# RWKV-7 products grouped by shape, heads in turn, with hand-over points between the groups

## The chip, the cores and the metric

The kernel runs on one core of one Trainium2 chip. The metric is device time in microseconds (us), as the median of repeated runs; smaller is better. TensorE (PE in the profile) multiplies matrices, VectorE (DVE) and ScalarE (ACT) work on elements, SyncE (SP) issues most DMAs.

## The reference, cut to what matters

A decoder trunk of two layers works on 1024 tokens of width 1024 in float32. Layer 0 mixes with gated linear attention and S5, layer 1 with RWKV-7 (8 heads of 64) and Mamba-2; each layer also has an input projection, an output projection and a gated MLP with a short convolution. The change is in RWKV-7 alone, whose recurrence is:

```python
def step(S, inp):
    rt, wt, kt, vt, at, bt = inp
    sa = jnp.einsum('bhij,bhj->bhi', S, at)
    S = S * wt[:, :, None, :] + sa[..., None] * bt[:, :, None, :] + vt[..., None] * kt[:, :, None, :]
    return S, jnp.einsum('bhij,bhj->bhi', S, rt)
```

## The kernel before, in words

The tokens are worked on in two halves of 512 (`h` = 0, 1). The layer products (projections and MLP, `fm_tile`, `project`) are made as three float32r products of a high and a low part each, 128x128 weights by 512 columns; they write to the four `acc` slots of PSUM. Each weight unit of 12 such products is followed by `tick(2.56)`.

The mixers are Python generators which run beside the layer products. `tick` (line 279) adds 2.56 us times a rate (0.7 for RWKV and Mamba) to a credit `due`, and lets the generator make steps, each up to its next `yield`, until the VectorE work that the steps traced (`cost`, counted in `tt`, `ts` and `stt` alone) has used up the credit. A step that has no such work costs nothing and is followed by the next in the same tick. `both` (line 228) advances two mixers together. This sets the program order; the framework that builds the program then puts the instructions of each engine into an order of its own, by their place in the program and by what is ready in its own reckoning, so that layer products fill in where a mixer's product would wait. Weight splitting and the evacuation of layer products carry a high priority.

RWKV-7 works on pairs of heads (4 pairs per half, 8 in all), tokens in 8 chunks of 64. `rwkv_pair` (line 1238) runs in this order:

- values without their mean into `SAV`, one product for the bonus (lines 1243 to 1255);
- the pairwise products inside a chunk (lines 1257 to 1268): per head and per half of the chunks (`q`) four products of 64 rows, 128 weight columns and 128 moving columns into one PSUM slot, then a masked copy by VectorE and a plain `yield`; head 0 first, then head 1;
- transposes, the inverse (30 VectorE steps), and `PV`;
- the recurrence over 8 chunks (lines 1292 to 1327): per chunk `pR`, `pS` and `pZ`, two products each, each answered by a small VectorE step;
- the output products (lines 1328 to 1335): per chunk and head one product of 128 rows by 64 columns (`SAV`, `Ph`) and one of 64 by 64 (`Zs`, `AR`), both added into the same place;
- squares and a copy by ScalarE, the sums over a head (`hsel`), a reciprocal root by way of DRAM, and the gate product `g2` (lines 1338 to 1358).

While a pair runs, `rwkv_prep` of the next runs with it in `both`. The mixers' PSUM slots are the four of `mx`. Every float32 product is two passes on TensorE, and so two matmul records in the trace.

Of the kernel before, what the change touches and what calls it, by code (L numbers as in the profile page):

```python
# [73 lines left out]

class Arena:
    """Fixed slots handed out in program order, the one that was freed first before the others."""
# [21 lines left out]
    def same(self, t, view):  # L98
        """Another view of a slot, which it is freed by from now on."""
        self.held[id(view)] = (self.held.pop(id(t))[0], view)  # L100
        return view
# [8 lines left out]
class Ring:  # L110
    """Fixed slots in turn."""
# [11 lines left out]
class Kernel:  # L123
    def __init__(self, ctx, tc, a, dump=None):
# [5 lines left out]
        # What the activation engine has just written, it also sends off.  # L130
# [68 lines left out]
    def paid(self, out):  # L199
        """Counts the vector engine's work, by which the mixers are traced among the products."""  # L200
        self.cost += 0.06 + float(np.prod(out.shape[1:])) / 960
# [26 lines left out]
    def both(self, a, b):  # L228
        """Two mixers in turn; the second's result."""
        left, res = [a, b], None  # L230
        while left:
            keys = []
            for g in list(left):
                try:
                    keys.append(next(g))
                except StopIteration as e:
                    left.remove(g)
                    if g is b:
                        res = e.value
            if keys:  # L240
                yield None if None in keys else keys[0]
        return res

    def staggered(self, gens, lead):
        """Mixers one after the other, each begun when the one before has made its first steps."""
        gens, live = list(gens), []
        while gens or live:
# [9 lines left out]
            if keys:  # L257
                yield None if None in keys else keys[0]
# [4 lines left out]
    def stats_beside(self, h):  # L263
        """The statistics of a norm in steps among the products that follow."""
# [14 lines left out]
    def tick(self, us):  # L279
        """After us of products: what runs beside them goes on by its share."""  # L280
# [7 lines left out]
        while self.side is not None and self.due > 0:  # L288
            c = self.cost
            try:  # L290
                if next(self.side) is not None:
# [3 lines left out]
                self.side = None  # L295
            self.due -= self.cost - c

    def drain(self):
        if self.side is not None:
            for key in self.side:  # L300
                assert key is None, key
# [5 lines left out]
    def tr(self, out, in_, shifted=False):  # L307
        """Transpose; to PSUM partitions that don't start at 0, a product with the identity."""
# [112 lines left out]
    def rsqrt_rows(self, src, scale, bias, op1):  # L421
        """(src scale op1 bias)^-1/2 of rows in PSUM, left in DRAM: spread over the partitions on the way."""
# [13 lines left out]
    def rows_to(self, t, rows):  # L436
        """Loads each row on its share of the partitions."""
# [5 lines left out]
    def norm_stats(self, h, t0=0, n=T, get=None, far=False):  # L443
        """1 / rms of n tokens, on every partition (far: spread there through DRAM) and with tokens on partitions."""
# [67 lines left out]
    def project_final(self, h, srcs, w, k0, nk):  # L512
        """The last products: half of the tokens first, so that their norm runs beside the others."""
# [32 lines left out]
    def ffn(self, h, l, at=None, mid=None):  # L546
        a = self.a
        last = h == NH - 1 and l == 1
        if last:
            # The first products don't wait for the norm: its factor comes with their results.  # L550
# [52 lines left out]
    def gla_decays(self, h, wa2, alo):  # L603
        """Cumulated log decays (times 16) inside each chunk."""
# [10 lines left out]
        # This one comes after every exponential: the logarithms then share one load of their table.  # L615
# [168 lines left out]
    def s5_prep(self):  # L784
# [72 lines left out]
        # phase table  # L857
# [29 lines left out]
        for half in range(2):  # L887
            hs = slice(4 * half, 4 * half + 4)
            power = lambda x, i: x[:, hs, i:i + 1].to_broadcast([128, 4, SC])
            # input matrices: transpose of A^{7-j} B'  # L890
# [14 lines left out]
            # output matrices C A^i (real part and minus the imaginary part), i = 1..8  # L905
# [7 lines left out]
            # kernels C A^tau B' and their Toeplitz matrices  # L913
# [28 lines left out]
    def s5(self, h):  # L942
# [23 lines left out]
        for ri in range(2):  # L966
            v = self.k2([128, 8, SN + 1])
            V.tensor_copy(v[:, :, 0], self.s5X[ri])
            # conj(phase) * V
# [80 lines left out]
    def proj0(self, h, at, mid):  # L1050
        a = self.a
        w = a["w0fm"]
        if h == 0:
            # The first products don't wait for the norm: its factor comes with their results.
# [34 lines left out]
    def proj0_vg(self, h, hd, xs):  # L1089
        """Values and gates of a head, tokens on partitions; with head 0 the forget gates' low rank."""  # L1090
# [34 lines left out]
    def gla(self, h):  # L1125
        a = self.a
        yield from self.need(("gla", h, 0))
        # [high, low, high] parts of the weights against [high, high, low] parts of the low rank
# [30 lines left out]
    def rwkv_keys(self, h):  # L1159
        """The keys, and the factors that normalise them."""  # L1160
# [13 lines left out]
    def rwkv_prep(self, h, pr, tw, rk):  # L1174
# [5 lines left out]
        # decay  # L1180
# [25 lines left out]
        # in-context rate  # L1206
# [7 lines left out]
        # keys  # L1214
# [14 lines left out]
        # receptance  # L1229
# [8 lines left out]
    def rwkv_pair(self, h, pr, sg, prep):  # L1238
# [3 lines left out]
        # The values go in without their mean over the head: the recurrence keeps it away from the outputs too.  # L1242
# [13 lines left out]
        # pairwise products inside a chunk  # L1256
        Ph = []
        for hh in range(2):
            P = self.k4([128, C8, 128])
            hs = slice(64 * hh, 64 * hh + 64)  # L1260
            for q in range(2):
                ps = self.mx([128, 4, 128])
                for c in range(4):
                    self.mm(ps[:, c], BK[hs, 4 * q + c].rearrange("p a b -> p (a b)"), AR[hs, 4 * q + c].rearrange("p a b -> p (a b)"))
                self.tt(P[:, 4 * q:4 * q + 4], ps, self.rwmask.unsqueeze(1).to_broadcast([128, 4, 128]), MUL)
                self.fr(ps)
                yield
            Ph.append(P)
# [18 lines left out]
        # recurrence over the chunks  # L1287
# [4 lines left out]
        for c in range(C8):  # L1292
# [34 lines left out]
            yield  # L1327
        ps = self.mx([128, C8, RC])
        for c in range(C8):
            z0 = h == 0 and c == 0  # L1330
            for hh in range(2):
                hs = slice(64 * hh, 64 * hh + 64)
                self.mm(ps[hs, c], SAV[:, c, hs], Ph[hh][:, c, 64:128], stop=z0)
                if not z0:
                    self.mm(ps[hs, c], Zs[hs, c], AR[hs, c, 1], start=False)
        self.fr(Zs, SAV, AR, BK, PV, *Ph)
        yield
# [4 lines left out]
        yield  # L1342
# [4 lines left out]
        yield  # L1347
# [12 lines left out]
    def rwkv_inverse(self, Ph):  # L1360
        """Writes (I - A)^-1 over the strictly triangular A in the blocks [0:64, c, 0:64] of Ph."""
# [61 lines left out]
    def conv4(self, h, i):  # L1423
        """Causal convolution and twice the SiLU of it."""
# [13 lines left out]
    def proj1_dt(self, h, xs):  # L1438
        """Step sizes before their bias: rows by the weights' high and by their low parts."""
# [50 lines left out]
    def decays(self, h, hd, p0=0, p1=128):  # L1490
        """Log decays of a head from the start of each chunk, on every partition."""
# [357 lines left out]
```

## Time and profile before

| what | value |
|---|---|
| median of 3 runs | 2851.04 us (2846.32 to 2853.56) |
| span of the profiled execution | 2840.4 us |
| TensorE busy | 2765.3 us (97%) |
| VectorE busy | 1857.5 us (65%) |
| ScalarE busy | 1133.0 us (40%) |
| mean granted TensorE clock | 0.968 |

Busy time is the time in which an engine had at least one instruction in work. [...] The span runs from the first to the last instruction; what lies around it (10.6 us between the span and the median) is outside the trace.

### The profile page before, as it was taken

How to read it: one execution, taken by the hardware profiler on the slowest of the kernel's cores; microseconds unless marked ns; L12 is line 12 of the kernel's file. 1: busy time of each engine (PE TensorE's matmuls, PEld its weight loads, DVE VectorE, ACT ScalarE, POOL GpSimd, SP SyncE). 2: the span in 40 equal slices, each digit the busy share in tenths (PEclk: the TensorE clock that was granted, in tenths of full speed). 3: DMA queues.
4: the chain of work that ended last, by engine and by line, in shares of the span. 5: the costliest groups of instructions: out<-in, count | busy, mean ns of one | idle time of the engine just before them, and what ended most of it. 6: DMA issues, size and time to landing. Idle time of an engine off the chain costs nothing.

```text
span 2840.4 us, 40016 instructions
## 1 busy us (share of the span) xinstructions
PE 2765.3 (97%) x14172; PEld 2178.2 (77%) x14172; DVE 1857.5 (65%) x4440; ACT 1133.0 (40%) x2035; POOL 2.1 (0%) x6
## 2 busy tenths in 40 slices
PE   8999999999999999999999899999999989999998
PEld 6878888888788776867776686867677677888886
DVE  6986378664557564848466775657575577767566
ACT  4553355442334333424234553333232354443333
POOL 0000000000000000000000000000000000000000
PEclk9999899998999999999999999999999999999998
DMA  6545554433334542424233455424232244434332
GB/s 214 183 144 165 161 161 119 121 96 122 100 101 141 178 134 78 127 68 110 70 80 117 115 163 173 134 79 116 77 94 74 73 127 133 135 99 124 97 97 86
DMA packets 275377, 339.79 MB, mean 120 GB/s; under 512 B 97764, under 2 KB 133284, under 8 KB 275176
## 3 DMA queue, kind: packets, MB, share of 16 engines
q1 hardware_dynamic: 274944, 337.07, 40.3%
q8 instruction: 111, 1.82, 0.3%
q14 instruction: 90, 0.74, 0.1%
q10 hardware_dynamic: 232, 0.17, 0.0%
HBM read 286.91 MB, written 49.63 MB: 118 GB/s over the span
## 4 chain that ended last, share of the span: by engine, by line
PE 65%; DMA 4%; DVE 3%; ACT 1%; issue 1%; SPq 0%; ACTq 0%; DVEq 0%
PE acc L305 54%; PE mx L305 11%; DMA k<-dr 3%; DVE k L218 1%; ACT k L204 1%; DVE wl L208 0%; PE mx L312 0%; DVE k L208 0%; DVE x L208 0%; DVE kf L218 0%; DMA dr<-sm 0%; DMA dr<-k 0%; DMA yl<-dr 0%; ACT wh L204 0%; DMA rb<-dr 0%
## 5 line engine op out<-in xcount | busy, mean ns | idle before, releaser
L204 ACT ACTIVATE wh<-wr 128x512 fp32r<-128x512 f32 (+1 forms) x802 | 496.2, 620 | 931.2 <-PE acc L305 781.5
L208 DVE TENSOR_TENSOR wl<-wr,wh 128x512 fp32r<-128x512 f32 (+1 forms) x800 | 540.5, 677 | 450.8 <-ACT wh L204 401.7
L305 PE MATMUL acc<-xh,wh 128*128 128x512 f32 x2000 | 798.3, 400 | 12.9 <-ACT xh L204 8.6
L305 PE MATMUL acc<-xl,wh 128*128 128x512 f32 x2000 | 794.3, 397 | 0.2 <-DVE xl L208 0.2
L305 PE MATMUL acc<-xh,wl 128*128 128x512 f32 x1984 | 785.7, 396 | 0.0
L305 PEld LDWEIGHTS acc<-xh,wh 128*128 128x128 f32 x2000 | 377.5, 189 | 108.3 <-issue 13.6
L305 PEld LDWEIGHTS acc<-xh,wl 128*128 128x128 f32 x1984 | 376.2, 190 | 83.2 <-issue 4.4
L305 PEld LDWEIGHTS acc<-xl,wh 128*128 128x128 f32 x2000 | 378.1, 189 | 80.6 <-issue 1.9
L305 PE MATMUL acc<-mh,wh 128*128 128x512 f32 (+1 forms) x972 | 383.7, 395 | 10.9 <-DVE x L208 7.0
L305 PE MATMUL acc<-ml,wh 128*128 128x512 f32 (+1 forms) x972 | 384.1, 395 | 0.0
L305 PE MATMUL acc<-mh,wl 128*128 128x512 f32 (+1 forms) x972 | 382.4, 394 | 0.0
L305 PEld LDWEIGHTS mx<-k,k 64*64 64x64 f32 (+5 forms) x2828 | 244.5, 152 | 115.4 <-issue 38.8
L305 PE MATMUL mx<-k,k 64*64 64x64 f32 (+10 forms) x2828 | 312.6, 260 | 9.9 <-DVE k L208 6.8
L208 DVE TENSOR_TENSOR k<-k,k 128x64 f32<-128x64 f32 (+27 forms) x894 | 283.8, 330 | 35.5 <-ACT k L204 18.4
L305 PEld LDWEIGHTS acc<-mh,wh 128*128 128x128 f32 x972 | 183.2, 189 | 52.5 <-DVE x L208 5.5
L305 PEld LDWEIGHTS acc<-mh,wl 128*128 128x128 f32 x972 | 183.4, 189 | 38.6 <-issue 1.9
L305 PEld LDWEIGHTS acc<-ml,wh 128*128 128x128 f32 x972 | 183.5, 189 | 38.3 <-issue 2.3
L204 ACT ACTIVATE k<-mx 128x512 f32<-128x512 f32 (+5 forms) x160 | 80.2, 511 | 257.0 <-PE mx L305 208.8
L204 ACT ACTIVATE k<-k 128x512 f32<-128x512 f32 (+3 forms) x176 | 108.7, 627 | 87.3 <-DVE k L208 47.5
L208 DVE TENSOR_TENSOR x<-acc,x 128x512 f32<-128x512 f32 (+1 forms) x172 | 107.2, 669 | 5.0 <-PE acc L305 4.9
L208 DVE TENSOR_TENSOR k<-k 128x256 f32<-128x256 f32 (+4 forms) x267 | 87.8, 355 | 25.4 <-DMA k<-dr 22.5
L218 DVE SCALAR_TENSOR_TENSOR kf<-acc,cols,kf 128x511 f32<-128x511 f32 (+1 forms) x132 | 98.2, 744 | 0.7
(174 smaller groups left out, 2273.0 us busy)
## 6 DMA issues: line engine op xcount, KB each, us to landing
wr<-wup SPq DMA_DIRECT2D x352, 256.0 KB, 2.6
wr<-wdn SPq DMA_DIRECT2D x176, 256.0 KB, 2.7
wr<-w1fm SPq DMA_DIRECT2D x104, 256.0 KB, 3.1
dr<-kf SPq DMA_DIRECT2D x72, 256.0 KB, 3.1
k<-dr SPq DMA_DIRECT2D x72, 256.0 KB, 3.8
yl<-dr SPq DMA_DIRECT2D x64, 256.0 KB, 2.8
wr<-wout SPq DMA_DIRECT2D x64, 256.0 KB, 2.7
wr<-w0fm SPq DMA_DIRECT2D x40, 256.0 KB, 3.0
```

The lines of the kernel that those rows point to most:

```text
L204: return self.A.activation(out, in_, f, **kw)
L208: return self.V.tensor_tensor(out, a, b, op=op)
L218: return self.V.scalar_tensor_tensor(out, a, s, b, op0=op0, op1=op1)
L305: return self.PE.matmul(out, lhsT, rhs, start=start, stop=stop)
```

## The change

It has four parts. A new mark `PAUSE` may be yielded by a mixer; `tick` then stops for this tick and keeps the credit that is left (a mixer that waits for data still loses it). `both` and `staggered` pass the mark on when either mixer gives it. The pairwise products go by halves of the chunks, with the two heads' products in turn, into two PSUM slots at a time. The output products go by halves of the chunks too: first all products of 128 by 64, then all of 64 by 64, heads in turn; the accumulation is started once for the whole slot. There are seven `yield PAUSE` per pair: two after pairwise groups, one before the output products, one after each half of them, one after the squares, and one after the reciprocal root. The rest of the diff takes out comments.

```diff
+PAUSE = "pause"
...
-                yield None if None in keys else keys[0]
+                yield self.joint(keys)
...
+    @staticmethod
+    def joint(keys):
+        return PAUSE if PAUSE in keys else None if None in keys else keys[0]
...
-                if next(self.side) is not None:
+                key = next(self.side)
+                if key is not None and key != PAUSE:
                     self.due = 0.0
                     return
             except StopIteration:
-                self.side = None
+                key = self.side = None
             self.due -= self.cost - c
+            if key == PAUSE:
+                return
...
-        Ph = []
-        for hh in range(2):
-            P = self.k4([128, C8, 128])
-            hs = slice(64 * hh, 64 * hh + 64)
-            for q in range(2):
-                ps = self.mx([128, 4, 128])
-                for c in range(4):
-                    self.mm(ps[:, c], BK[hs, 4 * q + c].rearrange("p a b -> p (a b)"), AR[hs, 4 * q + c].rearrange("p a b -> p (a b)"))
-                self.tt(P[:, 4 * q:4 * q + 4], ps, self.rwmask.unsqueeze(1).to_broadcast([128, 4, 128]), MUL)
-                self.fr(ps)
-                yield
-            Ph.append(P)
+        Ph = [self.k4([128, C8, 128]) for _ in range(2)]
+        for q in range(2):
+
+            ps = [self.mx([128, 4, 128]) for _ in range(2)]
+            for c in range(4):
+                for hh in range(2):
+                    hs = slice(64 * hh, 64 * hh + 64)
+                    self.mm(ps[hh][:, c], BK[hs, 4 * q + c].rearrange("p a b -> p (a b)"), AR[hs, 4 * q + c].rearrange("p a b -> p (a b)"))
+            for hh in range(2):
+                self.tt(Ph[hh][:, 4 * q:4 * q + 4], ps[hh], self.rwmask.unsqueeze(1).to_broadcast([128, 4, 128]), MUL)
+            self.fr(*ps)
+            yield PAUSE
...
+        yield PAUSE
         ps = self.mx([128, C8, RC])
-        for c in range(C8):
-            z0 = h == 0 and c == 0
-            for hh in range(2):
-                hs = slice(64 * hh, 64 * hh + 64)
-                self.mm(ps[hs, c], SAV[:, c, hs], Ph[hh][:, c, 64:128], stop=z0)
-                if not z0:
-                    self.mm(ps[hs, c], Zs[hs, c], AR[hs, c, 1], start=False)
+        both = [(slice(64 * hh, 64 * hh + 64), hh) for hh in range(2)]
+        for q in range(2):
+
+            cq = range(4 * q, 4 * q + 4)
+            for c in cq:
+                for hs, hh in both:
+                    self.mm(ps[hs, c], SAV[:, c, hs], Ph[hh][:, c, 64:128], start=c == 0, stop=False)
+            for c in cq:
+                for hs, hh in both:
+                    if h > 0 or c > 0:
+                        self.mm(ps[hs, c], Zs[hs, c], AR[hs, c, 1], start=False, stop=c == C8 - 1)
+            yield PAUSE
```

## Rows read from the trace of the kernel before

**Rows 1.** The page: span, and busy time of the engines.
```profile
span 2840.4 us, 40016 instructions
PE 2765.3 (97%) x14172; PEld 2178.2 (77%) x14172; DVE 1857.5 (65%) x4440; ACT 1133.0 (40%) x2035; POOL 2.1 (0%) x6
```

**Rows 2.** The page: the chain that ended last, shares by line.
```profile
PE acc L305 54%; PE mx L305 11%; DMA k<-dr 3%; DVE k L218 1%; ACT k L204 1%; DVE wl L208 0%; PE mx L312 0%; DVE k L208 0%; DVE x L208 0%; DVE kf L218 0%; DMA dr<-sm 0%; DMA dr<-k 0%; DMA yl<-dr 0%; ACT wh L204 0%; DMA rb<-dr 0%
```

**Rows 3.** Windows of eight pairs: start:end length, busy (instructions) per engine, clock, DMA.
```profile
sum 995.00, PE 994.34 PEld 730.42 DVE 611.63 ACT 334.17 POOL 0.00; mean PE 124.29 PEld 91.30 DVE 76.45 ACT 41.77 POOL 0.00
```

**Rows 4.** Windows of the eight pairs' output products.
```profile
1108.12:1117.50 9.38, 9.38 (x67) 6.80 (x65) 3.09 (x6) 0.57 (x1) 0.00 (x0) 0.71 0.00 0
...
2006.89:2018.50 11.61, 11.61 (x72) 8.36 (x68) 0.63 (x3) 0.00 (x0) 0.00 (x0) 0.63 0.10 23
...
sum 79.38, PE 79.38 PEld 57.56 DVE 11.11 ACT 3.36 POOL 0.00; mean PE 9.92 PEld 7.20 DVE 1.39 ACT 0.42 POOL 0.00
```

**Rows 5.** Timeline of PE, first pair: start, length, instructions, count.
```profile
1108.12 9.45 PE L305 MATMUL mx<-k,k 128*64 128x64 f32 x64
1117.50 2.07 PE L305 MATMUL mx<-k,ws 128*128 128x512 f32 x2
1119.50 1.86 PE L305 MATMUL mx<-k,cons 128*2 128x512 f32 x2
1121.30 1.58 PE L305 MATMUL mx<-cons,k 128*64 128x128 f32 x8
```

**Rows 6.** Timeline of PE, `PV`: one shape, one place in the array.
```profile
1045.95 2.08 PE L305 MATMUL mx<-k,k 64*64 64x64 f32 x32
1047.95 0.50 PE L305 MATMUL acc<-xh,wh 128*128 128x512 f32 x1
```

**Rows 7.** Windows from the outputs' end to the clock's return, eight pairs.
```profile
1117.50:1122.34 4.84, 4.84 (x10) 1.63 (x10) 0.69 (x1) 2.19 (x4) 0.00 (x0) 0.50 0.00 0
...
sum 37.12, PE 37.12 PEld 12.39 DVE 2.19 ACT 14.75 POOL 0.00; mean PE 4.64 PEld 1.55 DVE 0.27 ACT 1.84 POOL 0.00
```

**Rows 8.** Timeline of PE, one chunk of the recurrence (`pR`, `pS`, `pZ`) among layer products.
```profile
1091.72 0.33 PE L305 MATMUL mx<-k,k 64*64 64x64 f32 x4
1091.98 0.50 PE L305 MATMUL acc<-xh,wh 128*128 128x512 f32 x1
...
1092.65 0.44 PE L305 MATMUL mx<-r,k 64*64 64x64 f32 x4
1093.02 0.50 PE L305 MATMUL acc<-xh,wl 128*128 128x512 f32 x1
...
1093.90 0.34 PE L305 MATMUL mx<-k,k 128*64 128x64 f32 x4
1094.17 0.50 PE L305 MATMUL acc<-xh,wl 128*128 128x512 f32 x1
```

**Rows 9.** Timeline of PE: a float32 product of 512 columns at full clock.
```profile
1774.22 1.02 PE L305 MATMUL mx<-k,cons 128*128 128x512 f32 x2
1775.17 1.16 PE L305 MATMUL mx<-k,k 64*128 64x128 f32 x8
```

**Rows 10.** Windows of 19 stretches of pairwise products, `k` alone: length, PE, clock, DMA.
```profile
1006.93:1008.01 1.08, 1.08 (x9) 1.00 0.01 2
1016.40:1018.03 1.63, 1.63 (x16) 1.00 0.00 0
...
1256.45:1258.98 2.53, 2.53 (x24) 1.00 0.00 0
...
sum 29.83, PE 29.82; mean PE 1.57
```

**Rows 11.** Timeline of DVE: the masked copy of a group of pairwise products.
```profile
1128.20 0.69 DVE L208 TENSOR_TENSOR k<-mx,cons 128x512 f32<-128x512 f32 x1 [1.49 <-PE mx L305]
```

**Rows 12.** The chain in order of time: a long run of layer products.
```profile
767.94 114.27 PE acc L305 x504
```

**Rows 13.** Window between the last Mamba product and the layer's end, half 1.
```profile
2396.00:2467.00 71.00, 69.41 (x305) 56.63 (x303) 48.16 (x85) 33.27 (x57) 0.00 (x0) 1.00 0.50 157
```

More of the change, by code (lines that the diff above doesn't have):

```diff
@@ L257, in staggered @@
             if keys:
-                yield None if None in keys else keys[0]
+                yield self.joint(keys)
+    @staticmethod
+    def joint(keys):
+        return PAUSE if PAUSE in keys else None if None in keys else keys[0]
     def start(self, side, rate):
@@ L300, in drain @@
             for key in self.side:
-                assert key is None, key
+                assert key is None or key == PAUSE, key
             self.side = None
@@ L1327, in rwkv_pair @@
             yield
+        yield PAUSE
         ps = self.mx([128, C8, RC])
-        for c in range(C8):
-            z0 = h == 0 and c == 0
-            for hh in range(2):
-                hs = slice(64 * hh, 64 * hh + 64)
-                self.mm(ps[hs, c], SAV[:, c, hs], Ph[hh][:, c, 64:128], stop=z0)
-                if not z0:
-                    self.mm(ps[hs, c], Zs[hs, c], AR[hs, c, 1], start=False)
+        both = [(slice(64 * hh, 64 * hh + 64), hh) for hh in range(2)]
[9 more added lines that the diff above has]
+            yield PAUSE
         self.fr(Zs, SAV, AR, BK, PV, *Ph)
-        yield
         y, sq = self.k2(), self.k2()
@@ L1341, in rwkv_pair @@
         self.fr(ps)
-        yield
+        yield PAUSE
         ps = self.mx([2, T])
@@ L1346, in rwkv_pair @@
         self.fr(ps)
-        yield
+        yield PAUSE
         self.rows_to(sq, rows)
```

## The prediction, made before the result was known

> **What bounds the kernel now.** I read the engines' totals first, then the chain, then the stage that is changed. TensorE is busy in 2765.3 of 2840.4 us and no other engine above 65% [rows 1]; in the chain, 54% of the span are layer products and 11% the mixers' small products [rows 2]. So whatever the mixers take away from TensorE is paid by the whole kernel, provided that TensorE doesn't wait in their stage. It doesn't: over the eight head pairs of RWKV it is busy in 994.3 of 995.0 us, VectorE in 611.6 [rows 3]. A microsecond of TensorE saved there is a microsecond of the total, up to the 383 us in which VectorE is free.
>
> The stage is then read for what is dear in it. The eight stretches of output products take 79.4 us together 9.38 at a granted clock of 0.71 in the first and 11.61 at 0.63 in the longest [rows 4]. The first of them is 64 passes in 9.38 us without a layer product between [rows 5], 0.147 us a pass, where 32 passes of 64 columns that all have one shape take 2.00 us, 0.063 a pass [rows 6]. Two things make the difference. The two shapes (128 by 64 and 64 by 64) take turns, so that each product of two passes stands alone; and the clock falls to half in the middle of the stretch and stays there after its end, for 37.1 us more in the eight pairs [rows 7]. TensorE was not idle before it fell (9.38 of 9.38 us busy [rows 4]); what it did was the products of alternating shape and nothing else, and that is so in all eight.
>
> **Part 1, output products by shape.** What a group costs is read from one chunk of the recurrence [rows 8]: `pR` (two heads on different row halves) is 4 passes in 0.26 us, `pZ` (different column halves) 4 in 0.27, while `pS` (both heads in the same place) is 4 in 0.37. So two products in different halves of the array run side by side, and the 0.26 contains going into the shape and out of it. A further pass costs (2.00 - 0.37) / 28 = 0.058 us [rows 6, 8]. The new groups are 8 products each, 4 per head, 8 passes on either half: 0.265 + 6 x 0.058 = 0.61 us. Four groups per pair are 2.45 us, eight pairs 19.6, less 0.5 for the first chunk of half 0, which has no `Zs` product (2 passes a head fewer in each of 4 pairs, 4 x 0.12): 19.1 us. Today's 79.4 contain the last `pZ` (4 x 0.27, half 0) and the last `pS` (4 x 0.37, half 1) of the recurrences, so 76.8 are outputs. Gain 57.7 us. Bounds: if the halves don't run side by side over a long group, it takes 0.37 + 12 x 0.058 = 1.07 us, 32 groups 34 us, and the gain is 43.
>
> Both operands of a `pZ` product span all 128 rows and only their column halves differ, and yet the two cost 0.10 us less than the two of `pS` [rows 8]. [...]
>
> **Part 2, the clock.** With 2.45 us of outputs in four dense groups in place of 8 to 12 us of alternating ones, nothing like the work that preceded each fall is left. The 37.1 us at half clock [rows 7] are then done at full clock. A product of 128 by 512 takes 2.00 us there (1117.50 to 1119.50 [rows 5]) and 0.95 at full clock [rows 9]; the next one takes 1.80. I price the whole at one half: gain 18.6 us. Bounds: 0, if the clock falls all the same, to 18.6.
>
> **Part 3, pairwise products with the heads in turn.** Today they take 29.8 us in 19 stretches [rows 10]. Eight passes of one head take 1.08 us, and 24 passes take 0.90 more than 16, 0.11 a pass. A stretch of 16 in one place would be 1.08 + 0.90 = 1.98 us; the one of 1.63 crosses, by the program, from head 0 (rows 0 to 63) to head 1 (rows 64 to 127) once, and gains 0.35 us there, three passes side by side. With the heads in turn every pass has a partner, so a group of 16 costs what 8 cost, 1.08, and I take 1.1. Sixteen groups: 17.6 us, gain 12.2. Bounds: 1.98 each, no gain (a loss of 2), to 12.5. The group now holds two of four PSUM slots until two masked copies of 0.69 us [rows 11] are done, one after the other. Were TensorE to wait for both each time, it would be 16 x 1.4 = 22 us; I take 0, since today's copies are waited for in the same way and TensorE loses 0.7 us in 995 [rows 3], layer products filling in.
>
> **Part 4, the hand-overs.** Five of the seven marks per pair fall where no layer product runs today. A visit of two layer products between small ones takes 0.67 us (1091.98 to 1092.65 [rows 8]); in a long run they cost 114.27 / 504 = 0.227 each [rows 12], 0.45 for two. So a visit costs 0.22 us beside its work. If every mark lets layer products in, 5 x 8 x 0.22 = 8.8 us are lost. If the layer products that stand between the marks have already been used up as filling during the recurrence, which lets two to three in at each of its steps [rows 8], the marks change nothing and cost 0. I take the middle, 4.4 us.
>
> The credit that a mark leaves over is kept, so the mixers lose no pace; if they did, seven ticks for each of four pairs would be 28 x 12 x 0.227 = 76 us, against 71 us of layer products left after the last Mamba product [rows 13]. The reciprocal root's trip through DRAM (one transfer that ScalarE issues, four on SyncE's queue) comes later in the program by up to four ticks, behind as many weight loads on SyncE; nothing but its own pair's last copy waits for it, and that holds up no product. The early layer, where nothing yields the mark, keeps its order.
>
> **Sum.** 57.7 + 18.6 + 12.2 - 4.4 = 84.1 us. The profiled execution spans 2840.4 us, so the span after would be about 2756; the median of the runs is 10.6 us above the span, and I take that as unchanged: 2851.0 - 84.1 = 2767 us.
>
> **Rivals.** *The clock falls all the same*, since the small products after the outputs (gate, sums, next pair's values) still come in one run without layer products [rows 5]. Then part 2 is lost and a part of the outputs runs at half clock; a group of 0.61 us becomes at most 1.2, and if half of the 32 do, 10 us more: 2767 + 18.6 + 10 = 2796 us. For it: the run after the outputs is long today. Against it: those are 128-row products of 128 to 512 columns back to back, and in today's traces the clock comes back while they run (0.5 until 1122.34 [rows 7], which is inside the products from 1121.30 on [rows 5]). [...] Here the engine had no gap at all when it fell [rows 4].
>
> *The halves don't run side by side* over groups of 8, because the overlap reaches over a few passes alone: outputs 34 instead of 19 us and pairwise products as today, 2767 + 15 + 12 = 2794 us. Against it: three passes did overlap at a single crossing [rows 10], and with the heads in turn a product needs to reach over the two passes of the other head only.
>
> *The marks let credit pile up* (the one that ends slower). Five ticks without VectorE work add up to 5 x 1.79 = 9 us of credit, which is then let out in one tick: the next pair's preparation stands in one piece, its products wait for VectorE, and what is queued behind them on TensorE, layer products too, waits with them. It makes the kernel slower only if each pair waits more than 84 / 8 = 10.5 us, more than the whole piece; at 12 us a pair it would be 2863 us. Against it: VectorE is free 38% of the time [rows 3], and the order of the engines' queues is made so that layer products fill.
>
> *The marks come out empty and nothing else is lost*: 2763 us, inside my own range.
>
> **How the numbers follow.** Forecast (2756 to 2780, column halves and empty marks included): 0.78. Clock falls all the same (2780 to 2800): 0.11. No side by side: 0.04. More gained than priced, through waits that vanish in the Mamba stage behind it: 0.05. Slower: 0.02. The range reaches from 2752 to 2796, which leaves out about one in ten. A difference under 0.3% (8.6 us) can't be told from none by measurement. Every case but the last is faster by more than that: faster 0.96, same 0.02, slower 0.02.
>
> **What would show it.** In the changed kernel's trace: four groups of 16 passes per pair at about 0.6 us each; pairwise groups of 16 passes at 1.1; no stretch at 0.5 of the clock that begins in a pair's outputs, and a mean clock of about 0.98 or more in the RWKV windows; TensorE still busy without a gap there. It would be wrong if groups of 16 take over 1 us, if the falls stay, or if TensorE's waits on `mx` grow to tens of microseconds.

## The result and the profile after

The changed kernel took 2803.77 us (median of 4 runs, 2796.43 to 2807.50), the kernel before 2849.49 us beside it: a ratio of 0.9832 with an interval of 0.9806 to 0.9859. It is 1.7% faster, by 46 us; the forecast was 84, and 2803.77 lies above the upper end of the range (2796).

The page's head of the changed kernel, which answers to [rows 1]: TensorE is busy 64 us less, but the span is only 41.5 us shorter. The rest, 22 us, is new idle time of TensorE.

```profile
span 2798.9 us, 40033 instructions
PE 2701.4 (97%) x14172; PEld 2136.9 (76%) x14172; DVE 1863.6 (67%) x4440; ACT 1131.8 (40%) x2035; POOL 2.1 (0%) x6
```

**Output products.** The timeline of PE (start, length, instructions, count) for the outputs of the first pair, which answers to [rows 5]:

```profile
1107.17 2.91 PE L316 MATMUL mx<-k,k 128*64 128x64 f32 x62
1110.01 1.13 PE L316 MATMUL mx<-k,ws 128*128 128x512 f32 x2
1111.07 1.02 PE L316 MATMUL mx<-k,cons 128*2 128x512 f32 x2
1112.02 1.09 PE L316 MATMUL mx<-cons,k 128*64 128x128 f32 x8
```

62 passes in 2.84 us, 0.046 a pass in place of 0.147, still without a layer product between them; and the two products behind them take 2.01 us to the start of the next (1110.01 to 1112.02), where they took 3.80 at half clock. The eight stretches, with the last product of each recurrence, as windows (start:end length, then busy time and count of PE, PEld, DVE, ACT and POOL, clock, DMA; the clock is the granted TensorE clock as a share of full speed, 1.00 full, 0.50 half):

```profile
1106.40:1110.01 3.61, 3.61 (x69) 3.00 (x69) 0.56 (x2) 0.00 (x0) 0.00 (x0) 1.00 0.32 73
...
1962.65:1966.28 3.63, 3.63 (x74) 3.03 (x73) 0.81 (x4) 0.00 (x0) 0.00 (x0) 1.00 0.29 77
...
sum 26.90, PE 26.90 PEld 22.87 DVE 8.99 ACT 1.43 POOL 0.00; mean PE 3.36 PEld 2.86 DVE 1.12 ACT 0.18 POOL 0.00
```

The same stretches of the kernel before, counted from the same product, sum to 81.90 us (they begin one short group earlier than those of [rows 4]). All eight stand at a clock of 1.00 now.

**Pairwise products.** Windows of all 16 stretches of after, `k` alone (length, PE, clock, DMA), which answer to [rows 10]:

```profile
1013.22:1014.31 1.09, 1.09 (x17) 1.00 0.02 6
...
1117.25:1119.24 1.99, 1.99 (x24) 1.00 0.00 0
1138.84:1139.92 1.08, 1.08 (x8) 1.00 0.90 260
...
sum 22.84, PE 22.83; mean PE 1.43
```

A group of 16 costs 1.09, as worked out, but only in the first pair of each half. The other six pairs issue 24 passes at once and the last 8 follow 13 to 20 us later, as the kernel before did too (1256.45 in [rows 10]). The fourth block of 8 passes, one head alone, so has no partner, and neither has the third.

**What is new.** TensorE's waits between 990 and 2440 us (engine line, waited for: total, times, longest), first before, then after:

```profile
PE acc L305 <- DVE x L208: 9.0, 4, 3.9
PE mx L312 <- DVE k L218: 7.3, 4, 2.6
PE mx L305 <- DVE k L208: 5.6, 5, 1.8
```

```profile
PE acc L316 <- DVE x L212: 17.4, 7, 7.1
PE mx L316 <- DVE k L212: 10.6, 6, 2.3
PE mx L323 <- DVE k L222: 9.8, 5, 2.4
PE acc L316 <- DVE fcarry L588: 3.7, 2, 2.3
```

And the clock, as windows of the stretches at half clock (columns as above); there are seven between 990 and 2440 us, none of them in a pair's outputs:

```profile
1489.95:1496.78 6.83, 3.16 (x10) 2.53 (x11) 5.86 (x15) 1.53 (x3) 0.00 (x0) 0.50 0.17 58
2005.37:2012.20 6.83, 5.46 (x13) 4.31 (x14) 6.30 (x19) 0.32 (x1) 0.00 (x0) 0.50 0.17 52
2053.15:2059.98 6.83, 6.83 (x21) 3.65 (x21) 0.98 (x5) 0.71 (x3) 0.00 (x0) 0.50 0.12 40
...
sum 37.55, PE 32.52 PEld 22.82 DVE 24.58 ACT 8.57 POOL 0.00; mean PE 4.65 PEld 3.26 DVE 3.51 ACT 1.23 POOL 0.00
```

The first two belong to the two longest waits. This is the second one, in the timelines of PE and then of DVE:

```profile
2001.80 0.39 PE L316 MATMUL acc<-mh,wl 128*128 128x512 f32 x1
2006.73 0.79 PE L316 MATMUL acc<-xh,wh 128*128 128x512 f32 x1 [4.54 <-DVE x L212]
```

```profile
1995.32 0.69 DVE L212 TENSOR_TENSOR k<-mx,cons 128x512 f32<-128x512 f32 x1
1995.92 1.41 DVE L222 SCALAR_TENSOR_TENSOR k<-k,cols,k 128x512 f32<-128x512 f32 x2
...
2003.37 0.75 DVE L222 SCALAR_TENSOR_TENSOR k<-k,cols,k 128x512 f32<-128x512 f32 x1
2004.03 0.28 DVE L1392 COPY k<-k 32x256 f32<-32x256 f32 x1
...
2005.39 1.29 DVE L212 TENSOR_TENSOR x<-acc,x 128x512 f32<-128x512 f32 x2
```

A group of layer products ends at 2002.2. Its four sums have to be added to the residual `x` before the next group has their PSUM slots. VectorE is busy with hardly a gap (9.27 of the 9.37 us from 1996.00 to 2005.37), but mostly with the mixers' work, the next head pair's preparation above all (`k`), which stands in its queue from 1995.3 to 2005.4; 3.2 us of it, two weight splits (`wl`) among them, stand ahead of the additions when the group ends. TensorE waits 4.54 us and starts no other product in that time; the clock falls during the wait, 3.18 us into it, and the stretch at half clock lasts 6.83 us. The longest wait, 7.10 us up to 1493.62, is of the same kind, but in the Mamba stage behind the fourth pair: the group ends at 1485.4, its first addition starts at 1492.79, and ahead of it stand Mamba's steps, one of which waits 2.14 us for ScalarE.

The eight pairs alone, over two windows that answer to the 995.00 us of [rows 3]:

```profile
sum 917.00, PE 906.44 PEld 668.02 DVE 603.08 ACT 328.43 POOL 0.00; mean PE 453.22 PEld 334.01 DVE 301.54 ACT 164.22 POOL 0.00
```

TensorE is idle for 10.6 us there in place of 0.7, and four of the seven stretches at half clock (23.9 us) lie in them. Between 990 and 2440 us outside the pairs (Mamba, and the layer products about it) its waits grew from 28.6 to 39.0 us. All four waits for `x` in the kernel before lie there (1649, 2281, 2301 and 2415 us), none in a pair.

### The profile page after: what moved, and what is told of

It reads as the page before. It is cut to its first block, busy times and chain, and to the rows that moved or that the text cites. A ratio compares the mean times of both kernels' runs of the same rounds, so it can differ in the third digit from the quotient of the medians.

```text
span 2798.9 us, 40033 instructions
## 1 busy us (share of the span) xinstructions
PE 2701.4 (97%) x14172; PEld 2136.9 (76%) x14172; DVE 1863.6 (67%) x4440; ACT 1131.8 (40%) x2035; POOL 2.1 (0%) x6
## 4 chain that ended last, share of the span: by engine, by line
PE 60%; DMA 6%; DVE 5%; ACT 1%; issue 1%; SPq 0%; DVEq 0%; ACTq 0%
PE acc L316 51%; PE mx L316 8%; DMA k<-dr 4%; DVE k L222 1%; DVE k L212 1%; ACT k L208 1%; DVE wl L212 1%; DMA dr<-sm 0%; PE mx L323 0%; DMA yl<-dr 0%; DVE x L212 0%; DMA rb<-dr 0%; DVE kf L222 0%; DMA wr<-wup 0%; ACT wh L208 0%
## 5 line engine op out<-in xcount | busy, mean ns | idle before, releaser
L316 PEld LDWEIGHTS acc<-xh,wh 128*128 128x128 f32 x2000 | 378.2, 189 | 114.8 <-ACT xh L208 12.6
L316 PEld LDWEIGHTS mx<-k,k 128*64 128x64 f32 (+5 forms) x2828 | 201.9, 148 | 102.6 <-issue 44.7
L316 PE MATMUL mx<-k,k 64*64 64x64 f32 (+10 forms) x2828 | 252.1, 251 | 13.1 <-DVE k L212 11.5
```

The source lines that it names most:

```text
L316: return self.PE.matmul(out, lhsT, rhs, start=start, stop=stop)
```

## Experiments

All times are medians; the ratio is to the kernel before, measured beside it. The kernel before took 2849.49 us beside the changed kernel and 2842 to 2844 beside the others, so a difference of medians that involves the changed kernel at its own pace is uncertain by some 7 us. The letters A to F are those of the quoted expectations; "both" there means both regroupings.

**Which part loses: the change taken apart.** *shapes_only* has both regroupings, and each mark is a plain `yield` (the one before the output products is taken out):

```diff
-            yield PAUSE
+            yield
```

> Both regroupings of products, all marks turned into plain yields (the one before the output products taken out). Theory A (the products save what they were priced at, and the credit that the marks keep piles up VectorE work ahead of the layer's own copies, so that TensorE waits and the clock falls elsewhere): faster than the changed kernel by 10 to 30 us, 2775 to 2795, with TensorE's waits for the copies to x and the falls of the clock outside the outputs gone. Rival B (the losses come from where the mixers' steps happen to stand against the layer products, whatever the marks): within 10 us of the changed kernel, 2794 to 2814, with other waits in other places. Rival C (the marks hold the clock up): slower than the changed kernel by 10 us or more, with the clock falling at the outputs again.

Measured: 2787.92 us, 0.9814 [0.9791, 0.9838]. Without the marks 16 us of the missing 37 are back by the medians, 12.6 by the profiled spans and 5 by the ratios, whose intervals overlap; the rest is not. The time is the one that theory A expected, its sign is not there: TensorE still waits 16.0 us for `x` between 990 and 2440 us.

*marks_only* keeps both old orders and sets the seven marks (the last two, in place of plain `yield`s, are not shown here):

```diff
-                yield
+                yield (PAUSE if q == 1 else None)
...
+        yield PAUSE
...
+            if c % 4 == 3:
+                yield PAUSE
```

> The old orders of the products with seven marks per pair in the same places (after each head's pairwise products, after each half of the output products). Theory A: no gain on the kernel before, 2845 to 2870, the outputs still 8 to 12 us each and the clock falling in them. Rival C: layer products come between the halves, the clock stays up in half of the pairs or more, 2815 to 2835. Rival B: within 10 us of the kernel before, either way.

Measured: 2848.90 us, 1.0026 [1.0013, 1.0040]. The eight clock falls in the outputs are all there (102.4 us at half clock between 990 and 2440, as in the kernel before). So hand-overs alone neither hold the clock nor gain anything; they cost 0.26%, some 7 us.

*outputs_only* is the kernel before with the regrouped outputs:

```diff
+        for q in range(2):
+            cq = range(4 * q, 4 * q + 4)
+            for c in cq:
+                for hs, hh in both:
+                    self.mm(ps[hs, c], SAV[:, c, hs], Ph[hh][:, c, 64:128], start=c == 0, stop=False)
+            for c in cq:
+                for hs, hh in both:
+                    if h > 0 or c > 0:
+                        self.mm(ps[hs, c], Zs[hs, c], AR[hs, c, 1], start=False, stop=c == C8 - 1)
+            yield
```

> The kernel before with the output products alone regrouped, plain yields. By the priced terms: outputs 76.8 to about 22 us and 18 us for the clock, 2775 to 2785, if nothing is lost elsewhere (theory A, no marks, no loss). Rival B: 10 to 40 us of that are lost to waits elsewhere, 2790 to 2815.

Measured: 2771.58 us, 0.9751 [0.9726, 0.9776]. By the starts of the same layer products it gains 7.5 to 10.6 us at each of the eight pairs, 72.6 together; 2 us are lost ahead of the stage. That is parts 1 and 2 of the forecast (57.7 + 18.6 = 76.3) nearly whole, and the kernel is 32 us faster than the changed one (30 by the spans).

*pairwise_only* is the kernel before with the heads in turn in the pairwise products (the middle hunk of the diff, with `yield` for the mark):

> The kernel before with the pairwise products alone in turn, plain yields. Priced at 12 us less; in the changed kernel's trace six of eight pairs have 24 and 8 passes where two times 16 was meant, which is 7 us less. Theory A: 2837 to 2843, the same pattern of 24 and 8. Rival B: anywhere within 10 us of the kernel before.

Measured: 2855.35 us, 1.0050 [1.0030, 1.0070]: slower, though the products themselves take 22.9 us in place of 29.9. TensorE's waits between 990 and 2440 us are 38.4 us in place of 29.3, the half clock 122.9 in place of 102.4 (in the profile of a run of 2862.49 us). So far the pairwise products in turn looked like the culprit.

**Why would they cost: steps, slots or order.** On top of *outputs_only*, *turn_four_steps* has the heads in turn but hands over after each masked copy, so that a pair keeps its four steps (shown against the changed order, without the mark):

```diff
             for hh in range(2):
                 self.tt(Ph[hh][:, 4 * q:4 * q + 4], ps[hh], self.rwmask.unsqueeze(1).to_broadcast([128, 4, 128]), MUL)
-            self.fr(*ps)
-            yield
+                self.fr(ps[hh])
+                yield
```

> Outputs regrouped (no marks), and the pairwise products in turn with two PSUM slots, but with a yield after each masked copy, so that a pair again has four steps there and not two. Theory D (what costs is the number of steps: with two fewer, the next pair's preparation stands two steps earlier against this pair, and VectorE work comes thicker ahead of the layer's copies): the 16 us between outputs regrouped alone and both regrouped come back and the 7 us of the pairwise products are gained as well, 2762 to 2772. Theory E (two slots held at a time cost it): as with both regrouped, 2783 to 2793.

*old_two_steps* has the old order with one hand-over per head instead of two:

```diff
                 self.fr(ps)
-                yield
+            yield
```

> Outputs regrouped (no marks), the pairwise products in the old order, head after head, one PSUM slot at a time, but with one yield per head in place of two, so two steps as in the changed kernel. Theory D: 10 to 20 us slower than outputs regrouped alone, 2782 to 2792. Theory E: as outputs regrouped alone, 2767 to 2777.

*old_two_slots* has the old order too, but both slots of a head at once:

```diff
-                ps = self.mx([128, 4, 128])
+            ps = [self.mx([128, 4, 128]) for _ in range(2)]
...
-                self.fr(ps)
+            self.fr(*ps)
```

> Outputs regrouped, no marks, pairwise products head after head as before, but each head's two groups take two PSUM slots at once, both tiles taken at the start, one yield per head. It stands beside the same with one slot at a time (2777). Theory E, if the slots are what costs: 2787 to 2797. If the order of the products in turn is what costs, or placement: 2770 to 2784.

Measured: 2794.96 us, 0.9834 [0.9801, 0.9867]; 2777.45 us, 0.9767 [0.9745, 0.9790]; 2784.23 us, 0.9784 [0.9762, 0.9807]. Four steps don't help the new order and two don't hurt the old one by more than 6 us, so the number of steps is not it (theory D). Two slots at once cost 7 us more by the medians; the intervals overlap. The first lies above the ranges of both theories, the last below that of E. But each of these kernels also moves every later step of the mixers against the layer products, and that had not been tested by itself.

**The place of the steps.** The mixers' pace is one number; to change it moves all their steps and no work:

```diff
-RATES = [0.9, 0.35, 0.7, 0.7]
+RATES = [0.9, 0.35, 0.68, 0.68]
```

The same at 0.66 and 0.72, in four versions of the program.

> Outputs regrouped (no marks), and the mixers of layer 1 let in at a rate of 0.68 of the products' time and not 0.7: nothing but where the mixers' steps stand against the layer products. Rival B (placement alone moves the time by 10 us and more): 2780 to 2795 or under 2762. Theories D and E, in which the placement as such is worth little: 2766 to 2777.

> The same with a rate of 0.72. Rival B: 10 us or more from the 2772 of outputs regrouped alone, in either direction. Theories D and E: 2766 to 2777.

> Both regroupings without marks, rate 0.68 for layer 1's mixers. Rival B (placement: heads in turn only shift the next steps, by chance onto worse places at 0.7): the difference to outputs regrouped alone at the same rate (2766) is spread about the 7 us that the pairwise products save, so 2750 to 2770. Theory E (products in turn, two slots at a time, cost by themselves): 10 to 25 us over it again, 2776 to 2791.

> The same at a rate of 0.72, to be held against outputs regrouped alone at 0.72 (2783). Rival B: 2765 to 2788. Theory E: 2793 to 2808.

> The changed kernel, with the marks, at a rate of 0.68. Rival B: anywhere from 2765 to 2810. Theory E with marks at about 7 us: 2783 to 2798. Theory A (kept credit): as far above both regrouped without marks at 0.68 as at 0.7, 10 to 20 us.

> The kernel before at a rate of 0.68. If the slower rate by itself makes any version faster, 2825 to 2838, and the gains at 0.68 have to be read against that. If the place of the mixers is chance (rival B), anywhere within 10 us of 2843, and the gain of the change at 0.68 is 65 to 80 us.

> The changed kernel at a rate of 0.72, beside 2785 for both regrouped without marks and 2783 for outputs alone. Rival B: within 12 us of 2785, either way. Theory A (the marks' kept credit costs by itself): 2795 to 2805, as at 0.7.

> The changed kernel at a rate of 0.66. Rival B: 2760 to 2795, no order by rate. If a slower rate is better throughout, since it spreads the mixers' VectorE work: 2760 to 2770.

Measured, in us, with the ratios of the runs at another pace than 0.70:

| version | 0.66 | 0.68 | 0.70 | 0.72 |
|---|---|---|---|---|
| kernel before | | 2838.95, 0.9989 [0.9977, 1.0002] | 2842 to 2849 | |
| outputs regrouped | | 2765.85, 0.9727 [0.9708, 0.9746] | 2771.58 | 2783.39, 0.9788 [0.9767, 0.9809] |
| both regrouped, no marks | | 2768.88, 0.9738 [0.9720, 0.9756] | 2787.92 | 2785.01, 0.9789 [0.9771, 0.9807] |
| changed kernel | 2779.08, 0.9786 [0.9768, 0.9805] | 2770.11, 0.9735 [0.9716, 0.9753] | 2803.77 | 2807.10, 0.9875 [0.9852, 0.9899] |

At 0.68 the changed kernel takes 2770 us with every instruction of the change in it. That it is 3 us from the forecast is in part luck: the kernel before took 2842.68 us beside it, so the gain is 73 us of the forecast 84. The pairwise products in turn cost 16 us at 0.70, 3 at 0.68 and 2 at 0.72; the marks 16, 1 and 22. Counted in the traces, between the starts of layer products 3500 and 8000 (1005 and 2448 us in the kernel before), which leaves out the other stages, they are 12, 4 and -4 for the order and 14, -1 and 21 for the marks. Costs that come and go with the place of the steps are not fixed costs of the products or of the marks. (No line of [rows 1 to 13] could have shown this: they have one pace.)

The slower pace alone gives the kernel before nothing clear (0.9989). The place was no sure guide either: *outputs_rate68* (2765.85, against 2780 to 2795 or under 2762) and *after_rate72* (22 us from 2785, against 12) missed what rival B expected, and the second lies nearest to what theory A expected.

**What the place decides.** If it is the additions to `x` that stand behind the mixers' work on VectorE, then to let these go first, at the pace 0.70, must give the time back. *after_x_first*:

```diff
     def accumulate(self, h, grp, ps, t0=0, n=T):
...
-            with self.hp():
+            with self.tc.high_priority(offset=900):
                 self.tt(x, ps[o], x, ADD)
```

> The changed kernel at its own rate of 0.7, with a higher priority (900 in place of 300) for the layer's copies to x alone. If TensorE's waits for these copies, which stand behind the mixers' VectorE work, and the falls of the clock behind them are what the change loses at 0.7: these waits go from 17 us to under 8, and 2770 to 2792. If they are only a sign of something else: within 5 us of 2804.

Measured: 2781.08 us (2778.78 to 2785.75), 0.9795 [0.9778, 0.9813], 22.7 us less than the changed kernel by the medians (by the ratios 10.5, whose intervals overlap by a little). The profiles say the same as the medians: the span is 20.6 us shorter. The place shown above, now, PE and DVE:

```profile
1992.87 0.39 PE L316 MATMUL acc<-mh,wl 128*128 128x512 f32 x1
1996.11 0.50 PE L316 MATMUL acc<-xh,wh 128*128 128x512 f32 x1 [2.85 <-DVE x L212]
```

```profile
1993.92 0.68 DVE L212 TENSOR_TENSOR x<-acc,x 128x512 f32<-128x512 f32 x1
1994.52 0.74 DVE L222 SCALAR_TENSOR_TENSOR k<-k,cols,k 128x512 f32<-128x512 f32 x1
1995.18 0.27 DVE L1392 COPY k<-k 32x256 f32<-32x256 f32 x1
1995.38 0.67 DVE L212 TENSOR_TENSOR x<-acc,x 128x512 f32<-128x512 f32 x1
```

The additions pass the last of the preparation, and the wait is 2.85 in place of 4.54. Between 990 and 2440 us the waits for `x` go from 17.4 to 9.7 us, all waits from 49.0 to 38.1, the half clock from 37.5 to 17.1: 10.9 + 20.4 / 2 = 21.1 us of the 20.6. So waits and half clock make up the gain. That the waits for `x` are its main cause is not shown. They went to 9.7 us, not under 8, and give 7.7 us themselves. The two falls at the longest of them (13.7 us in all) give way to two at the same places (6.8 us), one half of which is 3.4 us; together 11 of the 21 us. The five other falls of the changed kernel go too, the two at 2053.15 and 2162.38 among them, which follow no wait, and three come elsewhere (10.2 us): so the edit moved more than those waits. At the pace 0.66 the changed kernel waits more for `x`, in seven waits of up to 8.2 us, and is 25 us faster than at 0.70:

```profile
PE acc L316 <- DVE x L212: 20.5, 7, 8.2
```

What is shown is that waits of all kinds and the falls of the clock together make the difference; the wait for `x` is the largest single one at 0.70.

**The same in two other places.** *outputs_68_x_first* has that line in the fastest version so far, *after_72_layer_first* in the changed kernel at 0.72, where part of the waits (8.4 us) are for the normalised copies `xl`, which go first as well:

```diff
             x = self.kf()
-            self.stt(x, self.X[h][k], self.col(name, k), self.rbc[h], MUL, MUL)
-            xs.append(self.split(x, self.xh, self.xl))
+            with self.tc.high_priority(offset=900):
+                self.stt(x, self.X[h][k], self.col(name, k), self.rbc[h], MUL, MUL)
+                xs.append(self.split(x, self.xh, self.xl))
```

> The kernel before with the outputs regrouped, the mixers' pace at 0.68 and the layer's additions to x ahead of the mixers' copies on VectorE. With the pace alone it took 2765.9 us, its waits of TensorE for x 9.0 us between 990 and 2440 us. Theory F (what is lost beside the direct terms is the waits for the layer's copies, and the clock that falls behind them): at most those 9 us are to be had, and the time is 2755 to 2766. Rival (the place of the mixers' steps decides, whichever copy goes first): the new order moves other copies back, and the time lies anywhere from 2760 to 2785.

> The changed kernel at pace 0.72, with the layer's additions to x and its normalised copies xl ahead of the mixers' copies on VectorE. Without that it took 2807.1 us, with 18.4 us of waits of TensorE for x and xl between 990 and 2440 us and 54.6 us at half the clock. Theory F: the waits fall to under 9 us, the half clock to under 30, and the time to 2775 to 2792. Rival (the cure at 0.70 was the luck of one place): no gain, 2800 or more. Rival (marks' kept credit costs by itself at this pace, 22 us): 2795 to 2803 at best.

Measured: 2765.02 us, 0.9718 [0.9693, 0.9742], no difference to 2765.85: the waits for `x` fall from 9.0 to 4.1 us, those for other copies grow by nearly as much. And 2800.65 us, 0.9843 [0.9813, 0.9873], 6 us less than at 0.72 without it. The first gained nothing; the second lies above theory F's range (2775 to 2792), though its waits for `x` and `xl` and its half clock fell as far as F expected. Waits of TensorE between 990 and 2440 us, first at 0.72 without, then with the layer's copies first:

```profile
PE acc L316 <- DVE x L212: 10.0, 7, 3.7
PE acc L316 <- DVE xl L212: 8.4, 2, 6.9
```

```profile
PE acc L316 <- DVE wl L212: 10.7, 9, 5.1
PE acc L316 <- DVE x L212: 5.8, 3, 4.6
```

All waits there fall from 49.2 to 40.6 us, the half clock from 54.6 to 13.7, and between layer products 3500 and 8000 this stretch (RWKV and Mamba) gains 71.5 us on the kernel before, where it gained 41.7. But the new line holds for the whole program, and ahead of RWKV, in stages that the change doesn't touch, it costs 24.7 us, 15.5 of them by layer product 1250 (394 us in the kernel before). Timeline of PE there with the line, then the window 330 to 420 us without it and with it:

```profile
355.33 3.78 PE L316 MATMUL mx<-k,ws 128*128 128x512 f32 x4 [8.89 <-DVE k L222]
364.57 0.79 PE L316 MATMUL acc<-mh,wh 128*128 128x512 f32 x1 [5.46 <-ACT mh L208]
```

```profile
330.00:420.00 90.00, 85.30 (x388) 70.50 (x387) 59.97 (x123) 48.09 (x85) 0.00 (x0) 1.00 0.60 188
```

```profile
330.00:420.00 90.00, 75.65 (x325) 61.43 (x324) 53.21 (x102) 39.87 (x70) 0.00 (x0) 0.89 0.46 142
```

So waits and clock account for the loss at 0.72 too, within these stages; as an edit of the whole program the cure moves the wait elsewhere. The line for these stages alone was not run.

**All versions in one sum.** From each profile I take the span, less TensorE's waits of over 0.2 us between 990 and 2440 us, less half of its time at half clock there (the two products behind the first pair's outputs took 3.80 us at half clock and 2.01 at full). What is left should depend on the products alone:

| kernel | span | waits | half clock | left |
|---|---|---|---|---|
| before | 2840.4 | 29.3 | 102.4 | 2759.9 |
| before_rate68 | 2838.9 | 27.3 | 102.4 | 2760.4 |
| marks_only | 2847.1 | 32.0 | 102.4 | 2763.9 |
| pairwise_only | 2860.7 | 38.4 | 122.9 | 2760.8 |
| outputs_only | 2769.1 | 30.6 | 17.1 | 2729.9 |
| outputs_rate68 | 2763.0 | 26.9 | 17.1 | 2727.6 |
| shapes_only | 2786.3 | 39.7 | 23.9 | 2734.7 |
| turn_four_steps | 2795.9 | 48.4 | 44.4 | 2725.3 |
| changed kernel | 2798.9 | 49.0 | 37.5 | 2731.1 |
| after_rate68 | 2767.9 | 32.5 | 23.9 | 2723.5 |
| after_rate72 | 2803.1 | 49.2 | 54.6 | 2726.5 |
| after_x_first | 2778.3 | 38.1 | 17.1 | 2731.7 |
| after_72_layer_first | 2799.0 | 40.6 | 13.7 | 2751.5 |

With the old outputs 2760 to 2764 us are left, with the new ones 2723 to 2735, though the spans of these differ by 40 us; the seven versions not in the table, all with new outputs, leave 2721 to 2734. The one exception is the last, which lost its time before 990 us. So what sets one version with new outputs apart from another is mostly waits and clock. The sum is no finer than some 14 us: it holds all that the other stages did (*shapes_only* is 8 us late at 1005 us), and the 7 us of the pairwise products don't show in it at 0.70.

## Why the prediction was wrong

**The step that failed** is a price of nothing. Part 3 took 0 for what the moved steps cost ("I take 0, since today's copies are waited for in the same way and TensorE loses 0.7 us in 995 [rows 3], layer products filling in"), and the sum then carried every microsecond saved on TensorE through to the end, on the word of [rows 3] that TensorE doesn't wait in this stage. That was a fact of the old placement, not a property of the stage. The cover was named (layer products) but not what the cover itself needs: an accumulator slot, which comes free only after an addition that shares VectorE's queue with the mixers (TensorE waited 17.4 us for these in the changed kernel). VectorE was free 38% of the time, and this I took for slack; what counts is what stands ahead of the additions when a group ends, and that was 3.2 and 7.4 us in the two longest cases. The sum also looked at the pairs alone, and half of the new waits came in the Mamba stage behind them, where the prediction saw only a chance of gains.

In numbers, from the profiles:

- *Output products*: 81.90 to 26.90, 55.0 us of a forecast 57.7. Right; the halves go side by side over groups of 8 products (16 passes in 0.615 us where only the column half differs, in 0.612 where the row half does too).
- *Clock behind the outputs*: no stretch at half clock begins in or follows a pair's outputs, and the products behind them are some 15.4 us shorter, of 18.6. Right.
- *Pairwise products*: 29.83 to 22.84, 7.0 us of 12.2. Right in the price of a group of 16, wrong in that all would be such groups: two pairs of eight have them.
- *Marks*: the layer products are used up when the outputs come, and none stands between the groups. As visits of layer products they come out empty, as the fourth rival had it: 0 us of 4.4 lost.
- *Sum of these*: 77.4 against a forecast of 84.1. Here 6.7 us of the missing 37 are.
- *What was priced at nothing*: waits between 990 and 2440 us 29.3 to 49.0, 19.7 us. Half clock outside the eight falls in the outputs (which last 81.9 us together): 102.4 - 81.9 = 20.5 us before, 37.5 after, at one half 8.5 us. Together 28.2. Some of the half clock is itself waiting (5.0 of the 37.5 us, 1.3 of the 20.5) and so is counted twice; without that it is 26.4, some 20.5 in the pairs and 6 behind them, where the half clock became less (20.5 to 13.7 us).

77.4 - 28.2 = 49.2 us, or 51.0 without the double count; by the layer products 3500 and 8000 the stage gained 47.2, so 2 to 4 us stay open. The profile of after is 6 us late at 1005 us, where both programs have issued the same products on TensorE. That leaves the 41.5 us between the spans.

**The rivals.** *The clock falls all the same* would have given 2796, nearest to what came, but its mechanism isn't what happened: it had the falls in the run of small products behind the outputs. The falls that came are elsewhere, and five of the seven begin in a wait of TensorE or up to 1.2 us behind one. At 1489.95 and 2005.37 TensorE had been waiting for 3.43 and 3.18 us; at 2053.15 and 2162.38 it had been busy in all of the 13.15 and 12.38 us before (below). *No side by side* fell with the first group of 16 at 0.61 us. *Credit piles up* had the right picture, mixers' work in one piece with the layer products held up behind it, but the wrong direction of the wait (the layer's additions stand behind the mixers' copies, not the mixers' products behind their own preparation) and a price of 12 us for every pair, where two places, only one of them in a pair, make 11.6 us of the waits. Whether the marks' kept credit is what made these pieces longer at 0.70 and 0.72 (14 and 21 us by the traces, against -1 at 0.68) was not separated from the place of the steps and stays open.

**What would have shown it.** TensorE's waits of before have 9.0 us for `x` between 990 and 2440 us, in four waits of up to 3.9, all behind the pairs. [rows 3] leaves them out, but they show the mechanism at work in this program. What costs 9 us in one placement can cost 3 or 20 in another, as the runs at other paces did. As a bound on the moved steps it would have put some 10 us of waits and as much again of clock on top of the 2767, some 2787, and the time still lay beyond that.

## What to carry to other kernels

Where an order is worked out once from priorities and a pace, an edit that changes the number or the place of a few steps also moves all later ones, and that alone was worth 18 to 37 us here in the three versions with new outputs, and nothing clear in the kernel before; time an edit at two or three paces before you judge it (at 0.70 the pairwise order and the marks looked like losses of 16 us each, at 0.68 of 3 and 1). When you say that other work covers a stall, ask what that work waits for itself, and which queue it shares with what you move. Output products that only differ in which half of the array they use, issued in turn, and those of one shape together, took 26.90 us here in place of 81.90; this part alone gave 60 to 78 us at the three paces.

The fastest versions run are the regrouped outputs alone at the pace 0.68, 2765.85 us (0.9727 [0.9708, 0.9746]), and the same with the additions first, 2765.02 us; both beat the kernel before and the changed one.

## What the runs showed of the hardware

**Column halves overlap as row halves do.** The groups of 16 passes 128 by 64, whose operands span all rows, take 0.615 us (1108.78 to 1109.40 in the trace of after), those of 64 by 64, which differ in the row half as well, 0.612; half of the 32 passes in one place of [rows 6] would be 1.00. No difference between the two shows here.

**The clock also falls without any idle time.** The fall at 2053.15 us of after follows this, in the timeline of PE and as a window:

```profile
2049.39 1.19 PE L316 MATMUL mx<-k,k 32*32 32x32 f32 x32
2050.52 0.50 PE L316 MATMUL acc<-xh,wl 128*128 128x512 f32 x1
...
2051.65 1.45 PE L316 MATMUL mx<-k,k 32*32 32x32 f32 x34
2053.02 0.70 PE L316 MATMUL acc<-xh,wh 128*128 128x512 f32 x1
```

```profile
2040.00:2053.15 13.15, 13.15 (x113) 10.67 (x112) 7.46 (x13) 5.72 (x10) 0.00 (x0) 1.00 0.50 123
```

TensorE was busy in 13.15 of 13.15 us, mostly with large layer products, and 64 passes of 32 by 32 were among the last (the last two passes of the group of 34 are of 64 by 64). The fall at 2162.38 follows the same sequence (12.38 of 12.38 us busy from 2150.00 on). The same small products stand in all eight pairs of both traces; no fall begins within 25 us behind them in the kernel before, and in the changed one none but these two. What decides between the two I have not found.
